# Weight roundings queued behind the PSUM evictions already written, and a layer's first two projections in the scores' banks

## The chip, the cores and the metric

The kernel runs on one core of a Trainium2 chip. The metric is the time of one execution on the device, in microseconds (us). The unchanged kernel ("before") was run three times: 1394.19, 1395.66 and 1396.37 us, median 1395.66.

A core has a matrix engine (TensorE, here PE), a vector engine (DVE), a scalar engine (ACT), GpSimd (POOL) and a sync engine (SP), which issues the large DMAs. Each takes its own instructions from its own queue in order, and waits for the others through semaphores. Matrix products accumulate in PSUM, eight banks of 128 partitions x 512 f32; everything else works from SBUF.

## The reference, cut to what matters

Two layers of an encoder over 512 tokens of width 1024, in f32:

```python
for l in range(2):
    h = rms_norm(x, norm_mix[l])
    q, k, v, gq, gk, gv = split(h @ w_in[l])            # 8 neighbourhood heads, 8 grouped queries on 2 KV heads
    na = neighbourhood_attention(q, k, v, rpb[l])       # softmax over windows of 8 rows x 16 columns
    ga = gqa_block_attention(rope(rms_norm(gq)), rope(rms_norm(gk)), gv)
    x = x + concat(na, ga) @ w_out[l]
    x = x + memory_cross_attention(rms_norm(x), rms_norm(mem), ...)   # 4 heads over 256 memory tokens
    x = x + conv_ffn(rms_norm(x), ...)                  # SwiGLU, width 2816, depthwise convolution of width 3
return rms_norm(x, norm_final)
```

## The kernel before

**Products in three parts.** Each f32 operand is held as two reduced-precision tiles (type F32R): `hi`, the rounded value, and `lo`, the rest. `mm3` forms a product as hi·hi + hi·lo + lo·hi, three matmuls into one bank. So a weight that comes by DMA (`raw`) must be rounded and its rest formed before PE can use it. This is `emit_split` (L249 to L266): `act.copy(hi, raw)` on ACT (L264, shown as `hi<-raw`) and `tensor_sub(lo, raw, hi)` on POOL or DVE (L265, `lo<-raw,hi`). Most weights of the attentions and all FFN weights are 128x1024; those of the attentions are cut in two, so a weight gives two copies and two subtractions of 128x512.

**When a weight is rounded.** `plan` lists all weights in the order of their use. `get_w` takes the next one and, on the way, calls `emit_split` for the one two places further on (five at most), and starts the DMAs of the next raw tiles. The program thus writes a weight's rounding well before its use, in the middle of the other work.

**What sets the order.** PE and SP keep the order in which the program writes their instructions. ACT, DVE and POOL do not: a planner places their instructions by a priority (the place in the program, moved by `behind(n)`) and by its own estimate of when operands are ready. Once the program is built, each engine's order is fixed. In before, a weight's rounding has `behind(45)`, so it may slide behind later work or stand ahead of it, as the planner finds ACT free.

**What takes results out of PSUM.** Most products leave their bank in the same two steps as the weights, hi on ACT and lo on DVE:

- `split_psum` (L469 to L475): softmax weights after their transposes (ACT L471, DVE L472) and v (L474, L475);
- `split_k` (L660 to L669): ACT L663, DVE L667; in layer 0's first key also a doubled copy;
- `split_q` (L678 to L683): ACT L681, DVE L683;
- `gqa_rope` (L831 to L889) for the grouped queries and the key: ACT L839 (times a gain) and L840 (square), DVE L841, then `swap` (a transposing product with `pairs` on PE, DVE L851 and L854), `rotate` (POOL L861 to L864), `norm` (a product with `ident` on PE, into a new bank) and `split` (DVE L874, then `split_q` or `split_k`).

A bank comes free when the last of these has read it.

**PSUM banks.** Three groups of tiles: `mm` with four banks (`ps_mm`), `sc` with two (`ps_s`, scores), `tr` with two (`ps_t`, transposes). A group hands its banks out in turn.

**The attentions.** In layer 0 `project_first` (L606) runs the first three projections q0, k0 and q1 interleaved, as x and the weights arrive; in layer 1 `project_qk` (L631) runs them one by one. Then come, woven together by hand-written schedules: the neighbourhood heads (`na_scores`, DVE L738 and ACT exponentials L744; `na_normalise`, L750, L756 and POOL L478; `na_transpose`; `na_values`, ACT L788 and DVE L789, L790), with the grouped projections as filler; then the grouped heads (`gqa_scores`, DVE L899 for the maximum and ACT L901 for the exponential; `gqa_normalise`, DVE L907 and POOL L478; `gqa_transpose_p`, transposes on PE and `split_psum`; `gqa_values`), with the output projection `out_na` (DVE L956 adds it to x) and the memory attention's preparation (ACT L539, L524; POOL L523; DVE L540) as filler. The memory attention and the conv-FFN follow. In time, layer 0's attention lies at about 25 to 241 us and layer 1's at about 705 to 924.

Of the kernel before, what the change touches and what calls it, by code (L numbers as in the profile page):

```python
# [12 lines left out]
AF = mybir.ActivationFunctionType  # L13
# [159 lines left out]
def encoder_kernel(ctx: ExitStack, tc: tile.TileContext, t: dict, out: bass.AP):  # L173
# [14 lines left out]
    @contextmanager  # L188
    def behind(n):


        at = tc.cur_priority
        tc.cur_priority = at + n
        yield
        tc.cur_priority = at
# [30 lines left out]
    ps_mm = lambda: ps("mm", 4)  # L226
# [5 lines left out]
    plan, raws, ready = [], [], []  # L232
    done = [0]

    def raw_tile():
        key, loads, nk, ncol, eng = plan[len(raws)]
        if eng[1:] == "x":
            raw = rtile((nk, ncol), F32)
        else:
            raw = wpool.tile([P, nk, ncol], F32, tag="raw", name=nm("raw"), bufs=N_RAW)  # L240
        raws.append(raw)
        return raw, loads
# [6 lines left out]
    def emit_split(act=ACT, cuts=2):  # L249
        n = len(ready)  # L250
        key, loads, nk, ncol, eng = plan[n]
        raw = raws[n]
        raws[n] = None
        if key[0] in ("up", "down", "memq", "memo"):
            cuts = 1
        if eng[1:] == "r":
            hi, lo = rtile((nk, ncol)), rtile((nk, ncol))
        else:
            hi = wpool.tile([P, nk, ncol], F32R, tag="hi", name=nm("hi"))
            lo = wpool.tile([P, nk, ncol], F32R, tag="lo", name=nm("lo"))  # L260
        with behind(W_BEHIND if done[0] and key[0] not in ("up", "down") else 0):
            for i in range(cuts):
                k = slice(nk * i // cuts, nk * (i + 1) // cuts)
                act.copy(hi[:, k], raw[:, k])  # L264
                (POOL if eng[0] == "P" else DVE).tensor_sub(lo[:, k], raw[:, k], f(hi)[:, k])  # L265
        ready.append((hi, lo))  # L266

# [200 lines left out]

    def split_psum(hi, lo, ps, scale=None):  # L469
        if scale is None:  # L470
            ACT.copy(hi, ps)  # L471
            DVE.tensor_sub(lo, ps, f(hi))  # L472
        else:
            ACT.mul(hi, ps, scale)  # L474
            DVE.scalar_tensor_tensor(lo, ps, scale, f(hi), op0=ALU.mult, op1=ALU.subtract)  # L475

    def normalise(e, sums, col, eng=DVE):
# [110 lines left out]
    for l in range(DEPTH):  # L588
# [11 lines left out]
        def project_first():  # L600

            w, pms = {}, {}
            for u, k0, k1 in ((0, 0, 2), (1, 0, 2), (0, 2, 4), (1, 2, 4), (2, 0, 4), (0, 4, 6),
                              (1, 4, 6), (2, 4, 6), (0, 6, 8), (1, 6, 8), (2, 6, 8)):
                if u not in w:
                    w[u], pms[u] = get_w(NA_ORDER[u]), ps_mm()  # L606
                if (u, k0) == (0, 0):

                    for k in range(2):
                        PE.matmul(pms[u], w[u][0][:, k], xg[k][0], start=k == 0, stop=False)  # L610
                        PE.matmul(pms[u], w[u][0][:, k], xg[k][1], start=False, stop=False)
                    for k in range(2):
                        PE.matmul(pms[u], w[u][1][:, k], xg[k][0], start=False, stop=False)
                    continue
                gemm_T(pms[u], w[u], xg, range(k0, k1), 0, KC - 1)
            load_bias(0)
            load_parameters()
            mix.stat()

            def evict():  # L620
                mix.spread()
                for u in range(3):
                    split_qk(*NA_ORDER[u], pms[u])

            late(1, evict)
            yield
# [2 lines left out]

        def project_qk(n, p):  # L630
            w = get_w((n, p))  # L631
            pm = ps_mm()
            gemm_T(pm, w, xg, range(0, 4), 0, KC - 1)
            yield
            gemm_T(pm, w, xg, range(4, 8), 0, KC - 1)
            if (n, p) == ("q", 0):
                mix.stat()
                held.append(pm)
            elif (n, p) == ("k", 0):
                mix.spread()  # L640
                split_qk("q", 0, held.pop())
                split_qk("k", 0, pm)
            else:
                split_qk(n, p, pm)
            yield
# [14 lines left out]
        def split_k(pm, kt, near):  # L660
            rows = [(slice(64 * j, 64 * j + 64), slice(64 - 64 * j, 128 - 64 * j)) for j in range(2)]
            for k, (r, o) in zip(kt, rows):
                ACT.copy(k[r, 0], pm[r])  # L663
                if near:
                    ACT.copy(k[o, 0], pm[r])
            for k, (r, o) in zip(kt, rows):
                DVE.tensor_sub(k[r, 1], pm[r], f(k[r, 0]))  # L667
                if near:
# [9 lines left out]
        def split_q(pm, st):  # L678
            halves = [(st[:, j], slice(64 * j, 64 * j + 64), slice(64 - 64 * j, 128 - 64 * j)) for j in range(2)]
            for v, r, o in halves:  # L680
                ACT.copy(v[r], pm[r])  # L681
            for v, r, o in halves:
                DVE.tensor_sub(v[o], pm[r], f(v[r]))  # L683

# [149 lines left out]
        def gqa_rope(g, pm):  # L834
# [2 lines left out]
            xs, sq, cc = tmp(), tmp(), tmp()  # L837
            with behind(-20):
                ACT.activation(xs, pm, AF.Copy, scale=gain)  # L839
                ACT.activation(sq, pm, AF.Square)  # L840
                DVE.scalar_tensor_tensor(cc, pm, gain, gtab[0][:, 0], op0=ALU.mult, op1=ALU.mult)  # L841

            def swap():
# [290 lines left out]
        ffn = nn  # L1134
# [222 lines left out]
```

## Time and profile before

| | |
|---|---|
| time, three runs | 1394.19, 1395.66, 1396.37 us (median 1395.66) |
| profiled execution | 1398.05 us |
| its span, first to last instruction | 1396.3 us |
| mean granted TensorE clock | 0.993 |
| busy PE, DVE, ACT, POOL | 1357.5, 832.4, 710.3, 719.2 us |
| HBM read, written | 125.00 MB, 2.10 MB |

The profile is one execution. In the lines quoted below, L264 is line 264 of the kernel; `out<-in` gives the tiles by the program's names. A timeline line has the start and the length in us, the engine, the line, the operation, the tiles and shapes, the number of instructions drawn together, and in square brackets how long the engine had been idle and what released it (the releaser is inferred). Where several instructions are drawn together the length is that of all of them.

### The profile page before, as it was taken

To read this page: it belongs to the slowest core of one execution; us is meant where nothing else is said; L and a number is where in the kernel's file an instruction comes from. 1 tells how busy PE (TensorE), PEld (TensorE's weight loads), DVE (VectorE), ACT (ScalarE), POOL (GpSimd) and SP (SyncE) were. 2 spreads that over 40 slices of the span, in tenths; PEclk is the share of its full clock that TensorE was granted. 3 is DMA by queue.
4 is the path that set the end of the run, shared out by engine and by line. 5 is a ranking of instruction groups with operands and counts; after the bars stand their busy time and mean duration, and the time that the engine had idled before them with its cause. 6 is when DMAs were issued, how large, how long until landed. Compare 5 with 4: busy or idle time off the path is not lost.

```text
span 1396.3 us, 19216 instructions
## 1 busy us (share of the span) xinstructions
PE 1357.5 (97%) x7088; PEld 1158.8 (83%) x7088; DVE 832.4 (60%) x1422; ACT 710.3 (51%) x1323; POOL 719.2 (52%) x537
## 2 busy tenths in 40 slices
PE   8999899989999999999999989999999999999997
PEld 7997789878888888888888878897788888888897
DVE  6666766364687178357446657753638843871873
ACT  6676577655443234234557657765554422432443
POOL 2458776634544443444645678756264444444441
PEclk9999999999999999999999999999999999999999
DMA  7653312422333333333355523223133333333331
GB/s 216 177 148 97 87 46 65 117 61 61 91 106 92 104 91 95 102 91 96 97 160 161 137 75 98 62 76 106 42 95 91 105 91 93 101 93 106 89 93 61
DMA packets 218205, 138.83 MB, mean 99 GB/s; under 512 B 6016, under 2 KB 211072, under 8 KB 218112
## 3 DMA queue, kind: packets, MB, share of 16 engines
q1 hardware_dynamic: 217968, 137.60, 34.3%
q8 instruction: 56, 0.92, 0.3%
q14 instruction: 37, 0.30, 0.1%
q10 hardware_dynamic: 144, 0.00, 0.0%
HBM read 125.00 MB, written 2.10 MB: 91 GB/s over the span
## 4 chain that ended last, share of the span: by engine, by line
PE 88%; DVE 4%; ACT 4%; issue 2%; DMA 1%; POOL 1%; SPq 0%; DVEq 0%; ACTq 0%
PE mm L76 80%; PE sc L76 3%; PE tr L63 3%; PE tr L76 1%; DMA raw<-in_w_in 1%; ACT hi L264 1%; DVE r L472 1%; ACT t L744 1%; POOL lo L265 0%; DMA xT<-in_xT 0%; ACT t L840 0%; DVE t L841 0%; DVE s L899 0%; ACT t L839 0%; DVE xg L472 0%
## 5 line engine op out<-in xcount | busy, mean ns | idle before, releaser
L265 POOL TENSOR_TENSOR lo<-raw,hi 128x1024 fp32r<-128x1024 f32 (+2 forms) x268 | 499.6, 1875 | 505.0 <-ACT hi L264 477.4
L76 PE MATMUL mm<-xg,hi 128*128 128x512 f32 x1984 | 617.1, 392 | 4.5 <-DVE t L841 2.9
L76 PEld LDWEIGHTS mm<-xg,hi 128*128 128x128 f32 x1984 | 369.9, 189 | 80.0 <-DVE t L841 3.3
L264 ACT CAST hi<-raw 128x512 fp32r<-128x512 f32 (+2 forms) x276 | 224.4, 836 | 345.0 <-PE mm L76 289.2
L76 PE MATMUL mm<-xg,lo 128*128 128x512 f32 x992 | 387.4, 391 | 0.0
L76 PE MATMUL mm<-r,hi 128*128 128x512 f32 (+1 forms) x1160 | 336.4, 374 | 2.5 <-DVE r L472 2.0
L76 PEld LDWEIGHTS mm<-r,hi 128*128 128x128 f32 x1160 | 210.5, 189 | 41.0 <-DVE r L472 2.8
L1181 DVE SCALAR_TENSOR_TENSOR t<-t,par,t 128x7 f32<-128x7 f32 (+1 forms) x352 | 201.9, 640 | 34.3 <-ACT t L1174 34.3
L76 PEld LDWEIGHTS mm<-xg,lo 128*128 128x128 f32 x992 | 187.0, 189 | 39.6
L76 PE MATMUL mm<-r,lo 128*128 128x512 f32 (+1 forms) x580 | 216.4, 373 | 0.0
L76 PEld LDWEIGHTS mm<-r,lo 128*128 128x128 f32 x580 | 109.4, 189 | 19.3
L1166 DVE TENSOR_TENSOR t<-mm,rep 128x512 f32<-128x512 f32 x88 | 60.1, 687 | 78.2 <-PE mm L76 61.9
L478 POOL TENSOR_SCALAR t<-t,s 128x512 f32<-128x512 f32 (+1 forms) x112 | 65.8, 602 | 77.8 <-DVE s L750 40.4
L1183 ACT ACTIVATE t<-t 128x512 f32<-128x512 f32 x44 | 27.9, 633 | 134.4 <-DVE t L1181 134.4
L1187 DVE TENSOR_TENSOR r<-t,r 128x512 fp32r<-128x512 f32 x44 | 90.2, 2051 | 7.3 <-ACT r L1186 4.1
L1210 DVE TENSOR_TENSOR xT<-xT,mm 128x512 f32<-128x512 f32 x32 | 21.9, 685 | 106.8 <-PE mm L76 106.8
L76 PE MATMUL sc<-r,r 128*128 128x256 f32 (+1 forms) x352 | 72.2, 336 | 4.1 <-DVE r L472 1.8
L63 PE MATMUL tr<-ident,t 128*128 128x128 f32 x456 | 62.9, 274 | 11.2 <-DVE r L472 3.8
L63 PEld LDWEIGHTS tr<-ident,t 128*128 128x128 f32 x456 | 52.3, 140 | 20.2 <-issue 7.9
L1174 ACT ACTIVATE t<-t,par 128x512 f32<-128x512 f32 x88 | 66.8, 806 | 3.3 <-DVE t L1166 3.3
L76 PE MATMUL mm<-r,r 128*128 128x256 f32 (+1 forms) x428 | 62.5, 297 | 0.0
L76 PEld LDWEIGHTS sc<-r,r 128*128 128x128 f32 x352 | 51.4, 190 | 10.0 <-ACT r L471 3.0
(136 smaller groups left out, 1541.8 us busy)
## 6 DMA issues: line engine op xcount, KB each, us to landing
raw<-in_w_up SPq DMA_DIRECT2D x88, 512.0 KB, 3.9
raw<-in_w_in SPq DMA_DIRECT2D x33, 512.0 KB, 4.6
raw<-in_w_down SPq DMA_DIRECT2D x32, 448.0 KB, 3.8
raw<-in_w_mem_kv SPq DMA_DIRECT2D x16, 512.0 KB, 3.9
raw<-in_w_down SPq DMA_DIRECT2D x16, 512.0 KB, 4.2
r<-in_bias SPq DMA_DIRECT2D x16, 384.0 KB, 5.6
r<-r SPq DMA_DIRECT2D x22, 256.0 KB, 5.3
raw<-in_w_out SPq DMA_DIRECT2D x8, 512.0 KB, 3.7
```

The costliest lines, as they stand in the source:

```text
L63: return lambda *a, **k: self.tc.keep_in_program_order(op(*a, **k))
L76: return self.tc.keep_in_program_order(self.engine.matmul(out, lhsT, rhs, **k))
L264: act.copy(hi[:, k], raw[:, k])
L265: (POOL if eng[0] == "P" else DVE).tensor_sub(lo[:, k], raw[:, k], f(hi)[:, k])
L472: DVE.tensor_sub(lo, ps, f(hi))
L478: eng.tensor_scalar(e, e, sums[:, col : col + 1], 1.0, op0=ALU.mult, op1=ALU.mult)
L1166: DVE.tensor_mul(u, us[side], ffn.rep)
L1174: ACT.activation(cc, u, AF.Identity, bias=par[:, l, CB + ch : CB + ch + 1], scale=w[1])
L1181: DVE.scalar_tensor_tensor(cc[:, dst], u[:, src], wi, cc[:, dst], op0=ALU.mult, op1=ALU.add)
L1183: ACT.activation(cs[0], cs[0], AF.Silu)
L1187: DVE.tensor_sub(acts[j][1], cs[0], f(acts[j][0]))
L1210: DVE.tensor_add(xT[m], xT[m], pm)
```

## The change

A dictionary `evicted` holds the last ACT eviction written so far of two kinds: "other" (from `split_psum`) and "projection" (from `split_k`, `split_q` and the square in `gqa_rope`). When a weight that is not one of the FFN's is rounded, each copy on ACT is written inside `tc.issue_after(e)` for both: on ACT's queue it must stand behind those evictions. This is an edge of order only, with no semaphore, since both ends are on ACT. The roundings of the FFN's weights ("up", "down") are left as they were.

Besides, the first two projections of a layer take their banks from the scores' group: q0 and k0 of `project_first` in layer 0, q0 and k0 of `project_qk` in layer 1 (there `p` is 0 for both).

```diff
@@ -232,6 +232,9 @@
     plan, raws, ready = [], [], []
     done = [0]
 
+
+    evicted = {}
+
     def raw_tile():
         key, loads, nk, ncol, eng = plan[len(raws)]
         if eng[1:] == "x":
@@ -258,10 +261,14 @@
         else:
             hi = wpool.tile([P, nk, ncol], F32R, tag="hi", name=nm("hi"))
             lo = wpool.tile([P, nk, ncol], F32R, tag="lo", name=nm("lo"))
-        with behind(W_BEHIND if done[0] and key[0] not in ("up", "down") else 0):
+        ffn = key[0] in ("up", "down")
+        with behind(W_BEHIND if done[0] and not ffn else 0):
             for i in range(cuts):
                 k = slice(nk * i // cuts, nk * (i + 1) // cuts)
-                act.copy(hi[:, k], raw[:, k])
+                with ExitStack() as after:
+                    for e in evicted.values() if not ffn else ():
+                        after.enter_context(tc.issue_after(e))
+                    act.copy(hi[:, k], raw[:, k])
                 (POOL if eng[0] == "P" else DVE).tensor_sub(lo[:, k], raw[:, k], f(hi)[:, k])
         ready.append((hi, lo))
 
@@ -468,10 +475,10 @@
 
     def split_psum(hi, lo, ps, scale=None):
         if scale is None:
-            ACT.copy(hi, ps)
+            evicted["other"] = ACT.copy(hi, ps).ins
             DVE.tensor_sub(lo, ps, f(hi))
         else:
-            ACT.mul(hi, ps, scale)
+            evicted["other"] = ACT.mul(hi, ps, scale).ins
             DVE.scalar_tensor_tensor(lo, ps, scale, f(hi), op0=ALU.mult, op1=ALU.subtract)
 
     def normalise(e, sums, col, eng=DVE):
@@ -603,7 +610,7 @@
             for u, k0, k1 in ((0, 0, 2), (1, 0, 2), (0, 2, 4), (1, 2, 4), (2, 0, 4), (0, 4, 6),
                               (1, 4, 6), (2, 4, 6), (0, 6, 8), (1, 6, 8), (2, 6, 8)):
                 if u not in w:
-                    w[u], pms[u] = get_w(NA_ORDER[u]), ps_mm()
+                    w[u], pms[u] = get_w(NA_ORDER[u]), ps_s() if u < 2 else ps_mm()
                 if (u, k0) == (0, 0):
 
                     for k in range(2):
@@ -629,7 +636,7 @@
 
         def project_qk(n, p):
             w = get_w((n, p))
-            pm = ps_mm()
+            pm = ps_mm() if p else ps_s()
             gemm_T(pm, w, xg, range(0, 4), 0, KC - 1)
             yield
             gemm_T(pm, w, xg, range(4, 8), 0, KC - 1)
@@ -660,9 +667,10 @@
         def split_k(pm, kt, near):
             rows = [(slice(64 * j, 64 * j + 64), slice(64 - 64 * j, 128 - 64 * j)) for j in range(2)]
             for k, (r, o) in zip(kt, rows):
-                ACT.copy(k[r, 0], pm[r])
+                e = ACT.copy(k[r, 0], pm[r])
                 if near:
-                    ACT.copy(k[o, 0], pm[r])
+                    e = ACT.copy(k[o, 0], pm[r])
+            evicted["projection"] = e.ins
             for k, (r, o) in zip(kt, rows):
                 DVE.tensor_sub(k[r, 1], pm[r], f(k[r, 0]))
                 if near:
@@ -678,7 +686,7 @@
         def split_q(pm, st):
             halves = [(st[:, j], slice(64 * j, 64 * j + 64), slice(64 - 64 * j, 128 - 64 * j)) for j in range(2)]
             for v, r, o in halves:
-                ACT.copy(v[r], pm[r])
+                evicted["projection"] = ACT.copy(v[r], pm[r]).ins
             for v, r, o in halves:
                 DVE.tensor_sub(v[o], pm[r], f(v[r]))
 
@@ -837,7 +845,7 @@
             xs, sq, cc = tmp(), tmp(), tmp()
             with behind(-20):
                 ACT.activation(xs, pm, AF.Copy, scale=gain)
-                ACT.activation(sq, pm, AF.Square)
+                evicted["projection"] = ACT.activation(sq, pm, AF.Square).ins
                 DVE.scalar_tensor_tensor(cc, pm, gain, gtab[0][:, 0], op0=ALU.mult, op1=ALU.mult)
 
             def swap():
```

The number of instructions of each engine stays the same, and so does PE's order.

## The prediction, made before the changed kernel ran

> **What bounds the kernel now.** I read the page first (busy times, chain of waits, groups), then the windows by stage, then PE's timeline for its gaps, then the other engines' timelines at each gap.
>
> ```profile
> PE 1357.5 (97%) x7088; PEld 1158.8 (83%) x7088; DVE 832.4 (60%) x1422; ACT 710.3 (51%) x1323; POOL 719.2 (52%) x537
> ...
> PE 88%; DVE 4%; ACT 4%; issue 2%; DMA 1%; POOL 1%; SPq 0%; DVEq 0%; ACTq 0%
> ```
>
> PE is busy 97% of 1396.3 us, and 88% of the last chain is PE's. The time can move only through PE's 38.8 idle us and through its clock. ACT, where the moved roundings run, is about half idle. The windows by stage (columns: length, then busy us of PE, PEld, DVE, ACT, POOL, the granted clock, DMA share) say where PE waits:
>
> ```profile
> 25.00:241.00 216.00, 204.34 (x1293) 182.39 (x1292) 139.71 (x294) 145.04 (x337) 141.32 (x157) 0.98 0.40 110
> ...
> 705.00:924.00 219.00, 211.18 (x1328) 188.10 (x1328) 135.10 (x289) 144.68 (x336) 141.21 (x156) 0.99 0.39 108
> ```
>
> The two attention stages, the only ones in which the change holds a rounding back for long, idle 11.7 and 7.8 of PE's 38.8 us. The conv-FFN, whose weights the change leaves out, lies between them. PE's timeline shows the gaps, layer 0 and then layer 1:
>
> ```profile
> 34.54 0.36 PE L76 MATMUL mm<-hi,xg 128*128 128x256 f32 x1 [1.85 <-DVE r L683]
> 120.81 0.50 PE L76 MATMUL mm<-xg,hi 128*128 128x512 f32 x1 [1.43 <-DVE t L841]
> 139.39 0.63 PE L63 MATMUL tr<-ident,t 128*128 128x128 f32 x4 [1.90 <-DVE r L472]
> 149.58 1.05 PE L76 MATMUL tr<-pairs,t 128*128 128x2 f32 x8 [1.32 <-ACT t L840]
> 164.41 0.63 PE L63 MATMUL tr<-ident,t 128*128 128x128 f32 x4 [1.67 <-POOL r L523]
> 166.21 0.73 PE L76 MATMUL sc<-r,r 128*128 128x512 f32 x2 [0.70 <-ACT t L901]
> ...
> 807.59 0.73 PE L76 MATMUL mm<-xg,hi 128*128 128x512 f32 x2 [1.43 <-DVE t L841]
> 826.17 0.52 PE L63 MATMUL tr<-ident,t 128*128 128x128 f32 x3 [1.91 <-DVE r L472]
> 837.96 0.38 PE L76 MATMUL tr<-pairs,t 128*128 128x2 f32 x2 [1.33 <-ACT t L840]
> 851.27 0.63 PE L63 MATMUL tr<-ident,t 128*128 128x128 f32 x4 [1.63 <-DVE xg L472]
> 851.65 1.18 PE L76 MATMUL sc<-r,r 128*128 128x512 f32 x4
> ```
>
> The same four places come back 686.8 us later. Call them A (34.54), B (120.81, 807.59), C (139.39, 826.17), D (149.58, 837.96) and E (164.41 to 166.21, 851.27). One thing more costs PE time, its clock:
>
> ```profile
> 151.00:154.00 3.00, 3.00 (x12) 2.57 (x11) 0.20 (x2) 0.00 (x0) 3.00 (x5) 0.52 0.53 131
> 826.97:830.38 3.41, 3.41 (x10) 2.63 (x9) 2.07 (x3) 1.51 (x3) 2.12 (x2) 0.50 0.09 20
> ```
>
> The granted clock is halved in these two stretches, and in a third of the same kind behind A. The second row is cut to its edges: 3.41 us at 0.50, about 1.7 us lost by each, some 5 in the profiled execution. Each comes right after a gap (A, D of layer 0, C of layer 1).
>
> **The change part by part.** Nothing is added or removed: the same roundings, evictions, matmuls and DMAs. PE's order is the same, SP's queue all but the same. What moves is the order on ACT, and through it on DVE and POOL, since the planner places them all. All three take their queues in order, so each moved instruction is a possible new wait. With the changed program's order beside the old one, I carried the durations of the rows through at A to E.
>
> *Roundings as such.* A pair takes about 1.14 us on ACT (the 135.53 and 147.19 rows below), its subtractions follow on POOL or DVE. Queued behind the evictions, weights come 2 to 12 us later; in before they are ready well ahead, and I found no first use overtaken. Cost taken 0; bounds 0 and +2.3 (one such pair of stretches, 1.14 each, late once). Cover gone, the matmul waits for that pair.
>
> *A, the banks.* With q0 and k0 in the scores' two banks, the third projection's successor (the first v block) finds a free bank, and the 1.85 us gap goes. But the first scores then wait for k0's last subtraction in that same bank, which was not on the path: v's block is done about 2 us earlier and the subtractions are not. The gap moves behind the v block. Bounds −1.85 and +0.3; I take −0.2, nearest to a mere move. In layer 1 there is no such gap, 0.
>
> *C and D: the intended gain.*
>
> ```profile
> 135.53 1.14 ACT L264 CAST hi<-raw 128x512 fp32r<-128x512 f32 x2 [1.75 <-PE mm L76]
> ...
> 147.19 1.14 ACT L264 CAST hi<-raw 128x512 fp32r<-128x512 f32 x2
> 148.35 0.69 ACT L839 ACTIVATE t<-mm,qkg 128x512 f32<-128x512 f32 x1
> 148.94 0.59 ACT L840 ACTIVATE t<-mm 128x512 f32<-128x512 f32 x1
> ```
>
> Here a rounding pair stands ahead of the rotary eviction L839/L840, which PE waits for directly (D), or over L841 and L472 (C). The change puts the pair behind. L839 then starts about where the pair started, which itself had waited for nothing but a 0.1 us overlap (D) or the projection's end (C). Of 1.14 I count −0.95 at D and −1.0 at C, in each layer.
>
> *B: a loss.* In the changed program the key eviction L663 stands ahead of the four exponentials L744 and of L839/L840; before, it came last.
>
> ```profile
> 117.30 0.48 ACT L744 ACTIVATE t<-sc,s 128x256 f32<-128x256 f32 x1
> ...
> 118.54 0.70 DVE L874 TENSOR_TENSOR mm<-t,mm 128x512 f32<-128x512 f32 x1 [0.45 <-PE mm L76]
> ...
> 121.44 1.41 DVE L667 TENSOR_TENSOR r<-mm,r 64x512 fp32r<-64x512 f32 x2 [0.68 <-ACT r L663]
> 123.33 0.68 DVE L789 TENSOR_TENSOR t<-mm,t 64x512 f32<-64x512 f32 x1 [0.48 <-POOL t L864]
> ...
> 120.23 1.17 ACT L663 CAST r<-mm 64x512 fp32r<-64x512 f32 x2
> 121.43 1.19 ACT L788 COPY t<-mm 64x512 f32<-64x512 f32 x2
> ...
> 124.48 1.16 PE L63 MATMUL tr<-ident,t 128*128 128x128 f32 x8
> ```
>
> L663 needs L874, done at 119.24, so ACT stands still until then: L663 pair to 120.4, three exponentials (0.47 each) to 121.8, L839 and L840 to 123.0, the last exponential and a rounding pair to 124.6, and L788 ends at 125.8 instead of 122.6. Behind it are DVE's two L789 (0.69) and the small L851 that frees the bank for PE's second transpose group: 126.85, where PE wanted it at 125.0 (half of the eight from 124.48). The stall at 120.81 itself becomes 1.1 longer (its bank is now freed by the two L667), but that is inside the 1.85. B: +1.9 per layer; bounds −1.4 and +2.5.
>
> *E: the largest term.* Before:
>
> ```profile
> 156.50 0.39 PE L76 MATMUL mm<-r,lo 128*128 128x512 f32 x1
> ...
> 155.38 1.17 ACT L681 CAST r<-mm 64x512 fp32r<-64x512 f32 x2 [4.52 <-DVE mm L874]
> 156.58 0.69 ACT L901 ACTIVATE t<-sc,s 128x512 f32<-128x512 f32 x1
> ...
> 158.01 0.69 DVE L956 TENSOR_TENSOR xT<-xT,mm 128x512 f32<-128x512 f32 x1
> 158.62 0.16 DVE L907 RECIPROCAL s<-s 128x2 f32<-128x2 f32 x1
> ...
> 158.87 1.36 POOL L478 TENSOR_SCALAR t<-t,s 128x512 f32<-128x512 f32 x2 [1.22 <-DVE s L907]
> ...
> 156.37 1.28 POOL L864 TENSOR_TENSOR t<-t,t 128x512 f32<-128x512 f32 x1
> ...
> 161.29 0.59 ACT L471 CAST xg<-tr 128x512 fp32r<-128x512 f32 x1
> 161.78 2.01 ACT L539 ACTIVATE r<-r 128x1024 f32<-128x1024 f32 x2
> ...
> 843.33 0.39 PE L76 MATMUL mm<-r,lo 128*128 128x512 f32 x1
> 846.06 1.84 POOL L523 TENSOR_SCALAR r<-r,par 128x256 f32<-128x256 f32 x4
> 848.64 0.71 ACT L524 CAST r<-r 128x256 fp32r<-128x256 f32 x2
> ```
>
> Changed order: on DVE the residual add L956, which must wait for the output projection's last matmul (156.89), stands ahead of L874; on ACT, L681 (needs L874) stands ahead of the exponentials L901; on POOL, L864 stands behind L478 of those exponentials; the next L874 needs that L864; and on ACT the next L681 and both L539 stand ahead of L471 and the next L901. From 156.89 this gives one chain: L956 0.69, L874 0.70, L681 1.17, L901 pair 1.36, L907 0.16, L478 pair 1.36, L864 1.28, L874 0.70, L681 1.17, L539 pair 2.01, L471 0.59, L901 0.69, L471 0.59, L901 0.69: 13.2, and some 0.4 of hand-overs, 13.6. The second score matmul, which needs the bank that the last L901 frees, would start at 170.5 where it started at 166.21: +4.3. In layer 1 the same chain has three L523 (0.46 each) ahead of L864 and two L524 (0.71) in place of L539, and one L471 less: 11.9 and 0.4, from 843.72 to 856.0, against 852.20 (half of the 1.18 after 851.65): +3.8. Bounds for each: −1.6 (the gap goes and no chain forms) and +5.5.
>
> *Clock.* I leave the three half-clock stretches as they are: those after C and D may go, two longer gaps at E may bring theirs. Bounds −5.1 and +3.4. The Trainium skill (TensorE: Matmul & The Clock Gate, What's actually happening) says that the window of 3413 ns runs free of the kernel and that the clock halves after at least one idle window. The length agrees with the 3.41 above; that an idle window is needed does not, since no gap here exceeds 1.91. By that rule only E's new gaps would halve the clock.
>
> *Sum.* Layer 0: −0.2 + 1.9 − 1.0 − 0.95 + 4.3 = +4.05. Layer 1: 1.9 − 1.0 − 0.95 + 3.8 = +3.75. Together +7.8 on the profiled execution's 1398.05 (span 1396.3), which is 2.4 above the median of the runs, 1395.66. The part that is the chip's phase (clock stretches) explains that much, so I add the sum to the median: 1403.5.
>
> **The rivals.**
> 1. *Faster: the chains at B and E don't form, C and D shrink.* For it: C and D point straight at roundings in ACT's queue. Against: in before, every start at E follows from in-order queues to within 0.05 us (L681 155.38 right behind L874, L901 156.58 right behind L681), so a changed order must bite. It decides if L956 or L681 comes earlier than I have it. Price: 2 × (−1.95) and up to one gap at E, −0.7: 1391.
> 2. *No change.* B and E lose just what C, D and the clock stretches give back, for instance E +1.2 each where POOL's L864 isn't the link that lasts: about +2.4 + 3.8 − 4.1 − 0.2, less a clock stretch: 1396.
> 3. *Worse: the clock follows.* Each gap over 3.4 us at E brings a half-clock stretch of 1.7 and the old ones stay, or a weight comes late: 1403.5 + 3.4 = 1407. By the skill's rule above it would be this one.
> 4. *The change doesn't do what it says.* The edge is only one of issue order and could leave the order alone; the orders differ in both attentions, so no chance of its own.
>
> **How the numbers follow.** A difference under 0.2% (2.8 us) can't be told from none here. Forecast (1400 to 1405.5) 0.54, rival 1 0.20, rival 2 0.12, rival 3 0.14. Faster 0.20, within 0.2% 0.12, slower 0.68. The likeliest case's own range is 1399 to 1407; to leave out no more than 2 in 10 it must reach into rival 2 and to the top of rival 3: 1393.5 to 1408. Predicted 1403.5.
>
> **What would show it.** In the changed profile: PE gaps at C and D about 1 us shorter; a gap over 3 us in front of a transpose or a score matmul at about 165 to 171 and 850 to 857, released by ACT t L901 or DVE xg L472; ACT idle before L681 there, released by DVE mm L874; ACT idle before L663 at about 118, released by DVE mm L874; the window 25 to 245 with over 14 us of PE idle. Wrong if E's gaps stay under 2 us, or if a matmul waits on POOL lo L265 or ACT hi L264.

## The result, and the profile after

| | before | after |
|---|---|---|
| median of the runs made together, us | 1396.01 (4 runs, 1394.19 to 1400.53) | 1415.18 (4 runs, 1412.52 to 1417.83) |
| ratio, with 95% interval | | 1.0123 [1.0104, 1.0142] |
| profiled execution, its span, us | 1398.05, 1396.3 | 1417.22, 1415.4 |
| mean granted clock of it | 0.993 | 0.987 |

The changed kernel is 1.2% slower, some 19 us. The forecast had the direction, 1403.5, but 1415.18 lies outside its range of 1393.5 to 1408.

The page of the changed kernel, busy times and the chain that ended last:

```profile
PE 1367.6 (97%) x7088; PEld 1166.6 (82%) x7088; DVE 834.7 (59%) x1422; ACT 710.2 (50%) x1323; POOL 720.0 (51%) x537
...
PE 84%; DVE 4%; POOL 4%; ACT 3%; DMA 3%; issue 2%; SPq 1%; DVEq 0%; ACTq 0%; POOLq 0%
```

The counts of instructions are those of before, and ACT and POOL are busy as long as they were. PE's idle time went from 38.8 to 47.8 us (1415.4 − 1367.6), and PE's busy time, for the same 7088 matmuls, from 1357.5 to 1367.6. So there are two losses of about 9 and 10 us: PE waits longer, and it works more slowly. In the chain POOL rose from 1% to 4% and DMA from 1% to 3%.

The windows of the changed kernel over the same two attention stages (columns as in the prediction):

```profile
25.00:241.00 216.00, 199.57 (x1236) 176.91 (x1235) 137.35 (x287) 139.91 (x324) 134.58 (x149) 0.98 0.38 105
705.00:924.00 219.00, 206.34 (x1217) 182.30 (x1217) 125.69 (x267) 133.43 (x307) 131.33 (x144) 0.96 0.37 106
```

PE idles 16.4 us of the first and 12.7 us of the second, where it had idled 11.7 and 7.8: 4.8 us more in each. The clock of the second stage fell from 0.99 to 0.96. PE's timeline in the changed kernel shows the gaps that answer to A to E, layer 0 and then layer 1:

```profile
122.77 0.70 PE L76 MATMUL mm<-xg,hi 128*128 128x512 f32 x2 [2.63 <-DVE r L675]
129.99 0.69 PE L63 MATMUL tr<-ident,t 128*128 128x128 f32 x4 [1.36 <-DVE s L859]
145.04 0.66 PE L63 MATMUL tr<-ident,t 128*128 128x128 f32 x4 [0.94 <-DVE r L479]
164.74 2.08 PE L76 MATMUL mm<-ident,t 128*128 128x128 f32 x8 [3.31 <-POOL t L870]
173.23 0.63 PE L63 MATMUL tr<-ident,t 128*128 128x128 f32 x4 [2.17 <-DVE xg L479]
...
780.92 0.36 PE L76 MATMUL mm<-hi,xg 128*128 128x256 f32 x1 [1.81 <-DVE r L482]
818.58 0.70 PE L76 MATMUL mm<-xg,hi 128*128 128x512 f32 x2 [2.63 <-DVE r L675]
860.72 0.70 PE L76 MATMUL mm<-ident,t 128*128 128x128 f32 x2 [3.47 <-POOL t L870]
870.08 0.50 PE L76 MATMUL sc<-r,r 128*128 128x512 f32 x1 [2.03 <-ACT t L909]
```

(Lines of the changed kernel are 7 to 8 further on than before's: its rounding is L271 and L272, the rotary eviction L847 and L848, `rotate` L869 to L872, the normalised product's DVE step L882, the transposes' eviction L478 and L479.) C fell from 1.90 to 0.94 (145.04) and D from 1.32 to 0.42. B rose from 1.43 to 2.63 (122.77), with a second gap of 1.36 behind it (129.99). E has 3.31 and 2.17 in place of 1.67 and 0.70. At 780.92, in the middle of layer 1's second v projection, stands a gap that the prediction didn't have (called the v block below; layer 0 has 0.59 at the same place, 86.66).

The same stretch of the other three engines at E of layer 0, in the changed kernel:

```profile
161.50 1.17 ACT L689 CAST r<-mm 64x512 fp32r<-64x512 f32 x2 [4.80 <-DVE mm L882]
...
160.12 0.69 DVE L964 TENSOR_TENSOR xT<-xT,mm 128x512 f32<-128x512 f32 x1 [0.53 <-PE mm L76]
160.72 0.69 DVE L882 TENSOR_TENSOR mm<-t,mm 128x512 f32<-128x512 f32 x1
...
167.30 0.70 DVE L882 TENSOR_TENSOR mm<-t,mm 128x512 f32<-128x512 f32 x1 [2.95 <-POOL t L872]
...
153.07 1.29 POOL L506 TENSOR_TENSOR r<-t,r 128x512 fp32r<-128x512 f32 x1 [1.08 <-ACT r L505]
154.38 1.28 POOL L871 TENSOR_TENSOR t<-t,r 128x512 f32<-128x512 f32 x1
...
156.17 2.53 POOL L272 TENSOR_TENSOR lo<-raw,hi 128x512 fp32r<-128x512 f32 x2
158.65 1.29 POOL L872 TENSOR_TENSOR t<-t,t 128x512 f32<-128x512 f32 x1
...
164.07 0.62 POOL L870 COPY t<-s 128x512 f32<-128x512 f32 x1
```

ACT stands still for 4.80 us ahead of L689, as forecast. DVE's L882, which it waits for, is queued behind the residual add L964, as forecast too; but its operand from POOL's L872 was itself done only at 159.94 (158.65 + 1.29), because a rounding's two subtractions (2.53) now stand in POOL's queue ahead of it. The add costs 0.8 there. From then on POOL is the late one: PE waits for its L870, done at 164.69, and the next L882 for its L872.

The remaining loss is the clock. Windows of the changed kernel, laid on the edges of the half-clock stretches: three pairs, each the 3.41 us ahead of a stretch and the stretch itself, and between them one window (171.38) that no half clock follows:

```profile
120.18:123.59 3.41, 0.82 (x4) 0.71 (x5) 1.38 (x2) 3.37 (x10) 2.08 (x2) 1.00 0.63 191
123.59:127.00 3.41, 3.41 (x10) 2.63 (x9) 0.83 (x2) 3.00 (x8) 1.34 (x2) 0.50 0.18 42
127.01:130.42 3.41, 2.05 (x19) 1.80 (x17) 2.11 (x5) 0.89 (x2) 3.41 (x5) 1.00 0.00 0
130.42:133.83 3.41, 3.41 (x10) 2.72 (x9) 2.41 (x4) 2.14 (x4) 3.30 (x3) 0.50 0.56 163
...
171.38:174.79 3.41, 1.56 (x9) 1.41 (x10) 2.95 (x6) 3.34 (x9) 3.41 (x8) 1.00 0.00 0
778.95:782.36 3.41, 1.60 (x14) 1.47 (x13) 0.48 (x1) 3.41 (x11) 2.92 (x3) 1.00 0.45 133
782.36:785.77 3.41, 3.41 (x18) 3.41 (x18) 2.45 (x5) 2.75 (x7) 2.21 (x4) 0.50 0.66 196
```

There are eight such stretches in this execution, from 123.59, 130.42, 164.55, 782.36, 819.91, 826.74, 860.87 and 871.11, against four of before (from 35.08, 151.13 and 826.97, and one at the start of the kernel, from 7.8). Each lasts 3.41 us at 0.50, so it loses about 1.7 us, and all starts lie on one grid: from 123.59 to 871.11 it is 219 steps of 3.413 us. The 3.41 us ahead of each of the eight hold a gap of PE, with 0.15 us (from 857.46) to 2.05 us (from 127.01) of work beside it. Before's stretch at the start cost little: after has none there, and its 101st matmul starts at 26.7 us where before's starts at 27.0. Both executions also end at half clock, from 1390.2 us in before and from 1407.0 in after, when PE has next to nothing left to do.

**The loss in two parts.** Every run has its span and its mean clock, so the clock's loss is span × (1 − clock): for the changed kernel 1413.4 × (1 − 0.9878) = 17.3 us, as means over its four runs. Span less this loss is called the rest here. Some 3 us of every clock loss (2.5 to 4.3 in the fourteen profiled executions) are the end of the execution, where half clock costs next to nothing; so of the two columns only differences are read. In the table, in us:

| kernel | runs | clock loss | rest |
|---|---|---|---|
| before (each batch of runs) | 15 to 23 | 7.1 to 8.1 | 1388.2 to 1388.4 |
| after | 4 | 17.3 | 1396.1 |
| banks only | 12 | 9.2 | 1388.8 |
| order only | 4 | 15.9 | 1395.0 |
| behind "other" only | 4 | 12.3 | 1397.8 |
| behind "projection" only | 4 | 16.3 | 1396.8 |
| POOL's steps behind the rotation | 4 | 17.7 | 1400.0 |
| output weights' rests on DVE | 4 | 13.8 | 1399.8 |
| first grouped weights free | 4 | 16.3 | 1396.7 |
| two weights only | 11 | 6.5 | 1388.2 |
| two weights, rests on DVE | 12 | 9.1 | 1388.6 |
| one weight | 12 | 9.7 | 1388.3 |
| after, gaps filled | 4 | 7.0 | 1399.3 |
| before, gaps filled | 12 | 5.1 | 1389.5 |

The rest scatters from run to run: four runs of one kernel lie within 1.9 us of each other at best and 7.9 at worst (output weights' rests on DVE), so a mean over four is good to one or two us. After less before (7.6 and 1388.2 in 23 runs): the rest grew by 7.9, the clock's loss by 9.7.

### The profile page after: what moved, and what is told of

It reads as the page before. It is cut to its first block, busy times and chain, and to the rows that moved or that the text cites. A ratio compares the mean times of both kernels' runs of the same rounds, so it can differ in the third digit from the quotient of the medians.

```text
span 1415.4 us, 19196 instructions
## 1 busy us (share of the span) xinstructions
PE 1367.6 (97%) x7088; PEld 1166.6 (82%) x7088; DVE 834.7 (59%) x1422; ACT 710.2 (50%) x1323; POOL 720.0 (51%) x537
## 4 chain that ended last, share of the span: by engine, by line
PE 84%; DVE 4%; POOL 4%; ACT 3%; DMA 3%; issue 2%; SPq 1%; DVEq 0%; ACTq 0%; POOLq 0%
PE mm L76 77%; PE sc L76 4%; PE tr L63 3%; POOL lo L272 2%; DMA raw<-in_w_in 1%; PE tr L76 1%; DMA t<-t 1%; ACT hi L271 1%; SPq L63 1%; POOL t L485 0%; DVE r L479 0%; DMA xT<-in_xT 0%; DVE xg L479 0%; DVE s L907 0%; POOL t L872 0%
## 5 line engine op out<-in xcount | busy, mean ns | idle before, releaser
L272 POOL TENSOR_TENSOR lo<-raw,hi 128x1024 fp32r<-128x1024 f32 (+2 forms) x268 | 500.2, 1877 | 541.7 <-ACT hi L271 519.7
L76 PE MATMUL mm<-xg,hi 128*128 128x512 f32 x1920 | 599.1, 393 | 5.3 <-DVE r L675 5.3
L76 PEld LDWEIGHTS mm<-xg,hi 128*128 128x128 f32 x1920 | 359.2, 189 | 77.8 <-issue 5.6
L76 PE MATMUL mm<-xg,lo 128*128 128x512 f32 x960 | 376.1, 392 | 0.0
L271 ACT CAST hi<-raw 128x512 fp32r<-128x512 f32 (+2 forms) x276 | 224.3, 840 | 301.0 <-PE mm L76 246.3
L76 PEld LDWEIGHTS mm<-xg,lo 128*128 128x128 f32 x960 | 181.6, 189 | 38.6
```

Source lines behind the costliest of these rows:

```text
L76: return self.tc.keep_in_program_order(self.engine.matmul(out, lhsT, rhs, **k))
```

## The experiments

Theories ahead of the runs: the order on ACT's queue causes it all, through DVE and POOL (the rival: the banks); POOL's order makes E's gaps (the rival: DVE's residual add); a rounding that waits for its DMA stands ahead of v's eviction; the half clock follows PE's gaps (the rival: it varies by itself). Each kernel had one profiled run and timed rounds beside before on the same chip.

**1. The banks alone.** The edges are taken out, the banks stay changed.

```diff
-                with ExitStack() as after:
-                    for e in evicted.values() if not ffn else ():
-                        after.enter_context(tc.issue_after(e))
-                    act.copy(hi[:, k], raw[:, k])
+                act.copy(hi[:, k], raw[:, k])
```

> The two bank lines alone; every engine's order stays that of before. Theory Q (the loss is the new order on ACT, DVE and POOL, and the clock follows the gaps it makes): within 3 us of before (1393 to 1399), PE idle 37 to 40 us, two to four half-clock stretches, and the 1.85 us gap ahead of the first v block gone or moved to the first scores. Rival B (the banks do it: the rotation of the four general banks shifts, and PE waits for a later reader at 120 us): over 1400, with the gaps at about 120 and 807 us above 2 us.

Measured 1399.34 against 1398.83, ratio 1.0012 [1.0000, 1.0023]. Its PE timeline behind the first v block:

```profile
36.99 0.38 PE L76 MATMUL sc<-r,r 128*128 128x256 f32 x1 [1.54 <-DVE r L669]
```

Before's gap of 1.85 at 34.54 is gone and two gaps, 1.54 and 1.14, stand behind the v block, in front of the first score products, which wait for the key's last subtraction in the bank that they need. The gap moved, as step A has it. The banks add at most 0.2%; they are not the cause.

**2. The order alone.** The banks are taken back, the edges stay.

```diff
-                    w[u], pms[u] = get_w(NA_ORDER[u]), ps_s() if u < 2 else ps_mm()
+                    w[u], pms[u] = get_w(NA_ORDER[u]), ps_mm()
...
-            pm = ps_mm() if p else ps_s()
+            pm = ps_mm()
```

> The queue edges alone, with all projections in the general banks; ACT's, DVE's and POOL's order is that of the changed kernel. Theory Q: as the changed kernel, 1411 to 1418, PE idle 46 to 50 us, gaps of about 2.6 us at 120 and 3.3 us at 161 and the same two in layer 1. Rival B: 1396 to 1404.

Measured 1412.53, ratio 1.0103 [1.0088, 1.0119]. Its PE timeline has the changed kernel's gaps, 2 us earlier in time:

```profile
120.55 0.81 PE L76 MATMUL mm<-xg,hi 128*128 128x512 f32 x2 [2.63 <-DVE r L675]
...
162.38 2.07 PE L76 MATMUL mm<-ident,t 128*128 128x128 f32 x8 [3.21 <-POOL t L870]
```

The edges alone carry the loss, as far as these runs can tell, and in both parts (rest 1395.0, clock loss 15.9).

**3 and 4. Only one kind of edge.** Behind the evictions of "other" alone, or of "projection" alone, with before's banks.

```diff
-                    for e in evicted.values() if not ffn else ():
+                    for e in [v for n, v in evicted.items() if n == "other"] if not ffn else ():
```

> As e2, but a rounding is held only behind the last eviction of transposes and v blocks, not behind projections. Theory Q with the losses shared by both kinds of edge: 1400 to 1409. If one kind carries the whole loss, one of e3 and e4 is at 1411 or more and the other within 3 us of before.

> As e2, but a rounding is held only behind the last eviction of a projection. At C and D it is the projection's eviction that the rounding stood ahead of, so the gaps at 137 and 148 us shrink by 1 us each as in the changed kernel. Theory Q with shared losses: 1400 to 1412; the gap at the residual add (about 161 us) over 2 us if the projection edge makes it.

Measured 1412.06, 1.0098 [1.0083, 1.0114], and 1415.22, 1.0122 [1.0100, 1.0144]. The loss isn't shared out between the two kinds: either one alone costs nearly the whole. PE's timeline with "other" alone, then with "projection" alone:

```profile
122.01 2.08 PE L76 MATMUL mm<-ident,t 128*128 128x128 f32 x8 [2.65 <-POOL t L870]
```

```profile
169.62 1.09 PE L63 MATMUL tr<-ident,t 128*128 128x128 f32 x4 [4.25 <-DVE xg L479]
```

Both disturb the same stretches, but in another way each: "other" alone makes PE wait for POOL at B (2.65, for a rotation's L870) and again at E, "projection" alone makes one long wait for ACT and DVE. So the loss does not hang on one of the two kinds; either gives the planner another order of the three engines. That is not so for every later rounding: with one or two weights (8 to 10 below) the waits cost nothing in sum.

**5. POOL's order at E.** If POOL's queue were only in a bad order, the rounding's subtractions and the normalised weights' (L506) could be held behind the rotation.

```diff
-                (POOL if eng[0] == "P" else DVE).tensor_sub(lo[:, k], raw[:, k], f(hi)[:, k])
+                with ExitStack() as after:
+                    if eng[0] == "P" and rot[0] is not None and not ffn:
+                        after.enter_context(tc.issue_after(rot[0]))
+                    (POOL if eng[0] == "P" else DVE).tensor_sub(lo[:, k], raw[:, k], f(hi)[:, k])
...
-                POOL.tensor_add(xr, cc, xr)
+                rot[0] = POOL.tensor_add(xr, cc, xr).ins
```

(and the same wrap around L506, `POOL.tensor_sub(lo, o32, f(hi))`.)

> The changed kernel, and on POOL each subtraction of a rounding (and that of a neighbourhood head's output) is held behind the rotation products already written. Theory P (at E POOL is late: a rounding's pair of subtractions, 2.5 us, and a waiting L506 stand ahead of the rotation that PE needs): the 3.3 us gaps at 161 and 857 us released by POOL shrink below 1 us, 4 to 9 us faster than the changed kernel with their half-clock stretches. Theory D (the residual add ahead of L882 on DVE, as predicted): the chain over ACT stays, a gap over 3 us at 161 to 172, at most 2 us faster.

Measured 1418.87, 1.0165 [1.0151, 1.0179]: slower still. Its PE timeline:

```profile
162.64 0.50 PE L76 MATMUL mm<-r,hi 128*128 128x512 f32 x1 [2.82 <-POOL r L512]
...
166.90 1.16 PE L76 MATMUL mm<-ident,t 128*128 128x128 f32 x8 [2.15 <-POOL t L876]
```

PE now waits for what was put back (L512 is the shifted L506), and for the rotation as well. In both orders that were tried POOL is late at E with something. The edge holds the subtractions back wherever a rotation has been written, not at E alone, so the time prices all of that; that this order of POOL mends nothing is shown, that no order would is not.

**6. Less work on POOL.** The rests of the output projection's weights go to DVE.

```diff
-            cols(("outn", mp), w_out, 0, 4, 256 * mp, 256, "P")
+            cols(("outn", mp), w_out, 0, 4, 256 * mp, 256, "D")
```

> The changed kernel with the rests (lo) of the four neighbourhood output-projection weights made on DVE (0.65 us each) instead of POOL (1.27 us): the queue edges stay, the 2.5 us of POOL ahead of the rotation go. Theory P: the gaps released by POOL at 161 and 857 us shrink by 2 us or more, 3 to 8 us faster than the changed kernel. Theory D: within 2 us of it, or slower, since DVE gets 1.4 us more ahead of L882.

Measured 1415.68, 1.0138 [1.0122, 1.0153], no gain. Its PE timeline at E:

```profile
172.17 1.22 PE L76 MATMUL sc<-r,r 128*128 128x512 f32 x2 [2.80 <-ACT t L909]
```

PE still waits for POOL, 2.62 in place of 3.31, and then longer for ACT, 2.80 in place of 2.17.

**7. The v block's gap.** The weights of the grouped key and of the first grouped query are left without edges.

```diff
-                    for e in evicted.values() if not ffn else ():
+                    for e in evicted.values() if not ffn and key not in (("g", "k"), ("g", 0)) else ():
```

> The changed kernel, but the weights of the grouped key and of the first grouped query are rounded without the edges. Theory M (in the second v projection a rounding waits on ACT for its DMA, 4.0 us in layer 1, and the eviction of v behind it holds PE's bank): the gaps at 86 (0.6) and 779 us (1.8) go, with the half clock after the second; 2 to 5 us faster than the changed kernel. If the v gap stays and no rounding waits there for a DMA, M is wrong.

The mechanism in the changed kernel itself first, at the v block of layer 1, ACT, DVE and then PE (whose row stands above, 780.92):

```profile
778.74 1.14 ACT L271 CAST hi<-raw 128x512 fp32r<-128x512 f32 x2 [3.96 <-DMA raw<-in_w_in]
779.79 0.47 ACT L481 ACTIVATE r<-mm,s 128x256 fp32r<-128x256 f32 x1
...
780.29 0.48 DVE L482 SCALAR_TENSOR_TENSOR r<-mm,s,r 128x256 fp32r<-128x256 f32 x1 [3.34 <-ACT r L481]
```

ACT stands 3.96 us in front of a rounding whose raw tile has not landed; behind it in the queue is v's eviction L481, then DVE's L482, and PE needs the bank that this frees. Measured: 1414.32, 1.0131 [1.0117, 1.0145]. In layer 0 the gap of 0.59 at 86.66 shrank to 0.30 (87.38), but at 81.43 one of 0.45 came, where PE waits for a weight's rest on POOL; in layer 1 it shrank from 1.81 to 1.44, but ACT waits as before:

```profile
777.27 1.14 ACT L271 CAST hi<-raw 128x512 fp32r<-128x512 f32 x2 [3.99 <-DMA raw<-in_w_in]
```

So the mechanism is visible, the cure was incomplete, and the time shows nothing of it. Whether the DMA could be made to start earlier, with one more raw tile, was not tried.

**8. Two weights alone.** Edges only for the two output weights that stood ahead of C and D, and before's banks.

```diff
-                    for e in evicted.values() if not ffn else ():
+                    for e in evicted.values() if key in (("outn", 2), ("outn", 3)) else ():
```

> The queue edges for two weights of each layer alone, the third and fourth of the neighbourhood output projection, which stand ahead of the rotary evictions at C and D in before; general banks. Gain theory: C and D shrink by 1 us each per layer and POOL keeps the rotation ahead: PE idle 34 to 36 us, 1390 to 1395. Theory P would let a gap at E grow by up to 2 us per layer, since the rounding's pair on POOL still moves: 1394 to 1400.

Measured 1396.37 against 1396.87, 0.9997 [0.9989, 1.0006]. In its PE timeline C fell from 1.90 to 1.63 and D from 1.32 to 0.41, but E grew:

```profile
155.18 1.16 PE L76 MATMUL mm<-ident,t 128*128 128x128 f32 x8 [0.77 <-POOL t L870]
163.25 1.08 PE L63 MATMUL tr<-ident,t 128*128 128x128 f32 x4 [3.29 <-POOL r L530]
```

What C and D give, E takes; the rest is before's 1388.2 to 0.1 us.

**9 and 10. Smaller still.** One weight alone, or these two with their rests on DVE, both with before's banks.

```diff
-                    for e in evicted.values() if not ffn else ():
+                    for e in evicted.values() if key == ("outn", 3) else ():
```

> The queue edges for one weight of each layer, the fourth of the neighbourhood output projection (D). The gaps at 148 and 837 us shrink by 0.9 us as in e5. If e5's new idle time at E came from the third weight's pair of subtractions, pushed on POOL from 136 us to behind the output projection, E stays as in before: PE idle 36.5 to 37.5 us, 1391 to 1395. If any rounding that leaves the rotary eviction's way meets it again at E, E grows by 1 us as in e5: 1394 to 1398.

> e5 with the rests of these two weights made on DVE, not on POOL. If POOL is what E waits for, E's growth in e5 (+1.5 and +1.2 us) goes and C's and D's gain stays: PE idle 35 to 37 us, 1391 to 1395. If E is bound by the chain over ACT and DVE, DVE's extra 1.4 us per weight makes it no better than e5: 1395 to 1399.

Measured 1400.60, 1.0018 [1.0008, 1.0029], and 1399.28, 1.0014 [1.0006, 1.0023], both a little slower. Their rest is before's (1388.3 and 1388.6); what grew is the clock's loss, 9.7 and 9.1 against 7.6. With one weight D is again 0.41 and a gap of 2.08 comes at E. With the rests on DVE, POOL's gaps at E are 0.30 and 1.66, and in layer 0 DVE is late in POOL's place:

```profile
176.90 0.98 PE L76 MATMUL tr<-ones,t 128*128 128x1 f32 x4 [5.90 <-DVE s L915]
```

**11. The changed kernel with its gaps filled.** PE gets idle matmuls (512 columns, into a transposes' bank that nobody reads) in front of the grouped v projection, 10, and of the last query's product with `ident`, 12, in each layer. The waits stay; PE is busy in them.

```diff
+    FEED = InOrder(tc, nc.tensor)
...
+        def feed(n):
+            d = ps_t()
+            for _ in range(n):
+                FEED.matmul(d, xg[0][0][:, 0:P], xg[0][0], start=True, stop=True)
...
+            if g == "v":
+                feed(10)
...
+                if g == 3:
+                    feed(12)
```

> The changed kernel with idle matmuls put on PE where it waits: 10 of 512 columns ahead of the grouped v projection (the 2.63 us gaps at 120 and 816 us) and 12 ahead of the last query's norm product (the 3.3 us gaps at 161 and 857), into a transpose bank that nobody reads. They add about 2.3 and 2.8 us of work that fits into the waits. Theory C (a half-clock stretch follows a gap of PE): the stretches right after these four gaps (124, 165, 820, 861) go, up to four of the eight, so 3 to 7 us faster than the changed kernel although the waits themselves stay. Rival R (the stretches come with the code there or at random): as many stretches, the time within 2 us of the changed kernel or longer.

Measured 1407.92, 1.0082 [1.0054, 1.0109]; some 6 to 7 us faster than the changed kernel (the two intervals overlap by a hair, 1.0104 to 1.0109) with 44 matmuls more (the two groups of layer 0 take 2.46 and 2.88 us, so about 10.7 us in all). Its PE timeline and its windows over the two stages:

```profile
118.13 2.46 PE L63 MATMUL tr<-xg 128*128 128x512 f32 x10
120.92 0.70 PE L76 MATMUL mm<-xg,hi 128*128 128x512 f32 x2 [0.34 <-DVE r L676]
...
156.34 2.88 PE L63 MATMUL tr<-xg 128*128 128x512 f32 x12
160.13 1.16 PE L76 MATMUL mm<-ident,t 128*128 128x128 f32 x8 [0.92 <-POOL t L878]
```

```profile
25.00:241.00 216.00, 204.67 (x1296) 181.56 (x1297) 141.36 (x293) 143.06 (x333) 139.79 (x154) 1.00 0.38 108
705.00:924.00 219.00, 211.10 (x1300) 186.70 (x1299) 134.56 (x284) 139.79 (x323) 134.19 (x149) 0.99 0.37 104
```

The waits are there, worked through instead of idled: B's 2.63 became 2.46 of idle matmuls and 0.34 of wait, E's 3.31 became 2.88 and 0.92. The half-clock stretches of the profiled execution went from eight to one (from 859.57), and over the runs the clock's loss went from 17.3 to 7.0, which is before's, while the rest rose by 3.2.

Of the seven stretches that went, four had followed the gaps now filled (123.59, 164.55, 819.91, 860.87). The one at the v block of layer 1 went together with its gap, though nothing was put there: ACT waits 1.13 us for the DMA there in place of 3.96, so the order on the engines changed as well. The two behind B's second gap went although that gap stayed (1.35 at 126.53 and at 816.84). The one that is left follows a gap of 2.09 (858.34) that was not filled. So a filled gap draws no half clock, and a gap that stays may or may not; some 10 us of clock loss went with the fill, not all of it provably by the fill.

**12. Before with its gaps filled.** The same for the unchanged kernel: 7 idle matmuls in front of layer 0's first v block (A), 5 in front of the last query's product with `pairs` (D) in each layer (`feed` is given the bank here).

```diff
+            if (l, g) == (0, 0):
+                feed(ps_t(), 7)
...
                 pv = ps_t()
+                if g == 3:
+                    feed(pv, 5)
```

> The kernel before, with idle matmuls on PE in two of its own waits: 7 ahead of layer 0's first v block (the 1.85 us gap at 34 us) and 5 ahead of the last query's sum of squares in each layer (the 1.3 us gaps at 149 and 838 us). Theory C: the half-clock stretches that follow 34 and 149 us in before (35 and 151) go, 1.7 us each, and the fill costs nothing while it fits into the wait: 1.5 to 4 us faster than before, 1393 to 1397 against 1397 to 1398 of the runs beside it. Rival R: no fewer stretches, the same time, or slower by the fill's 0.2 us per matmul (up to 4 us).

Measured 1396.16 against 1398.51, 0.9989 [0.9980, 0.9997]: the lowest ratio of all, 0.1% under before, which is just clear of the noise, and about 19 us under the changed kernel. Its PE timeline at A, and windows where before had its stretches of layer 0, with the one that is left:

```profile
32.42 1.75 PE L63 MATMUL tr<-xg 128*128 128x512 f32 x7
34.72 0.36 PE L76 MATMUL mm<-hi,xg 128*128 128x256 f32 x1 [0.55 <-DVE r L684]
```

```profile
35.00:38.40 3.40, 3.19 (x27) 2.98 (x25) 3.06 (x5) 3.33 (x6) 2.26 (x2) 1.00 0.34 102
...
140.49:143.90 3.41, 3.41 (x10) 2.67 (x9) 2.07 (x3) 1.47 (x3) 2.15 (x2) 0.50 0.09 19
151.00:154.40 3.40, 3.20 (x22) 2.71 (x21) 1.27 (x4) 1.72 (x5) 3.40 (x4) 1.00 0.34 77
```

Full clock behind A and D, and one stretch behind C, which was not filled (in before it was C of layer 1 that had one, not C of layer 0). The idle matmuls cost 1.1 us of the rest and spare 2.7 of clock loss.

## Why the prediction was right or wrong

The delays between the same matmuls of both profiled executions, added up by place, stand beside its terms:

| step | predicted, us | wait measured, layer 0 and layer 1 |
|---|---|---|
| A, the banks | −0.2 | about 0 |
| roundings as such | 0 (bounds 0 and +2.3) | +0.74 and +1.38, at the v blocks |
| B | +1.9 each | +2.44 and +2.55 |
| C and D | −1.95 each | −1.86 and −1.87 |
| E | +4.3 and +3.8 | +2.95 and +3.75 |
| clock | 0 (bounds −5.1 and +3.4) | +9.7 in the runs |

**The waits.** A, C and D came as worked out. B has the mechanism of the prediction (ACT stands 5.68 us in front of the key's eviction, released by DVE's L882), a little dearer:

```profile
120.01 1.17 ACT L670 CAST r<-mm 64x512 fp32r<-64x512 f32 x2 [5.68 <-DVE mm L882]
```

The gap in front of the v projection grew by 1.20 (to 2.63), as the step had it (1.1). The second gap, in front of the transposes, is 1.36, where the step's 1.85 left 0.75 for it. DVE's two evictions of the values (L797, before's L789) were to start behind ACT's L796; by the releaser that the profile names they started only when PE's products with `pairs` had ended, and L859, which frees the bank, stands behind them:

```profile
128.25 1.40 DVE L797 TENSOR_TENSOR t<-mm,t 64x512 f32<-64x512 f32 x2 [3.55 <-PE tr L76]
```

E's size is right in layer 1 and 1.35 too high in layer 0, and its chain is half right. The step began the chain with the residual add, which is there but costs only 0.8; the link that lasts is POOL's, whose rotation stands behind a waiting subtraction and a rounding's pair. The prediction had listed L864's place behind L478 but not that pair. Its sign, a gap over 3 us in front of a transpose or a score matmul, released by L901 or L472, did not come: the gaps over 3 us (3.31 and 3.47) stand in front of the product with `ident` and are released by POOL's L870. Only the smaller ones behind them (2.17 and 2.03) have the releasers it named. In layer 1 the steps it lists add up to 12.7, not 11.9 (13.2 + 3 × 0.46 − 2.01 + 0.71 − 0.59), which would have made the term +4.6; that +3.8 came so near +3.75 is in part luck.

"Roundings as such" at 0 failed at the v blocks: it looked for a first use overtaken, and the loss is that the rounding itself waits, for its DMA (2.56 us in layer 0, 3.96 in layer 1), with v's eviction behind it.

All terms together gave +7.8 and the rest grew by 7.9, but that match is luck: the waits in the table add up to +10.1, some −0.7 came later, and PE's idle time grew by 9.0. B and the roundings were too low and E too high, and the rest is good to one or two us only.

**The step that failed** is the clock: "I leave the three half-clock stretches as they are". The term was 0 with +3.4 as its bound, and the runs showed +9.7: the loss grew from 7.6 to 17.3. (In the two profiled executions it is eight stretches of 1.7 us against three that cost, +8.5.) That is most of the 11.7 us between 1403.5 and 1415.2. Rival 3 named the mechanism, but let only the gaps over 3.4 us at E bring a stretch. The rows of before already spoke against this: its own gaps of 1.85, 1.32 and 1.91 had each brought one, while others of 1.33 to 1.90 had not. Every new or longer gap should have had a stretch as its upper bound: two at E, two at B (one for each of its gaps), in both layers, and one or two at the v blocks, each 1.7. In the profile of after seven of the eight stretches lie at B and E and one at a v block. That a gap of PE draws them is shown by experiments 11 and 12: the four behind the gaps filled in 11 went, as did before's two at A and D in 12, and the clock's loss over the runs fell by 10.3 and 2.7. How many of the new ones are the doing of a gap alone is not shown, since in 11 three others went without a fill.

The forecast of a stalled ACT ahead of L681 and L663 and of over 14 us of PE idle in the first stage held; it said that the reasoning would be wrong if E's gaps stayed under 2 us, and they are 3.31 and 2.17. Its other sign of being wrong, a matmul that waits for a rounding's rest (L265, now L272), came once, for 0.15 us at 80.42.

**The clock rule.** In the changed kernel half clock came after 3.41 us windows that held between 0.15 (857.46) and 2.05 us (127.01) of PE work, and on one grid. The Trainium skill (TensorE: Matmul & The Clock Gate, What's actually happening) has the clock halve after at least one idle window of about 3.4 us, in a window that runs free of the kernel. The grid and the length agree with the rows. That the window must be idle does not: 1.36 us of idle was enough at 127.01. If idle means wholly idle, no half clock would have followed any of the windows shown.

**Left open.** How E's loss divides among POOL, DVE and ACT: each of experiments 5, 6, 9 and 10 took or shortened one wait there and found another. The DMA wait at layer 1's v block, which no run took away by itself. And what decides whether a gap is followed by half clock.

## What to carry to other kernels

A rounding moved on one in-order queue can take its other half on POOL or DVE, its raw tile's DMA and the planner's order of all engines with it, and a wait taken away at one engine can come back at the next, as it did here at E. When a change may open a gap of over a microsecond on a matrix engine that is 97% busy, price the gap together with the half-clock stretch that can follow (here 1.7 us each, in all about as much as the waits themselves). Where a wait can't be removed, a few idle matmuls in it can cost less than the clock that they keep (experiment 12: 1.1 us against 2.7).

## What the runs showed of the hardware

Half clock came after windows of the 3.41 us grid with only 1.3 to 2 us of idle PE, and not always. Two windows of before, the first followed by half clock and the second not:

```profile
147.72:151.13 3.41, 2.09 (x14) 1.58 (x13) 2.46 (x6) 3.12 (x8) 3.41 (x4) 1.00 0.16 36
...
161.37:164.78 3.41, 1.74 (x13) 1.32 (x12) 3.33 (x6) 3.41 (x6) 1.85 (x5) 1.00 0.00 0
```

The second has less PE work and kept its clock, as did the changed kernel's 171.38 (1.56). So busy time alone does not decide; what does, these runs do not settle. Nor does the same program have the same stretches in every run: of 23 runs of before the shortest span, 1391.8 us, had a mean clock of 0.997 and the longest, 1398.1, one of 0.992, and the span less the clock's loss scattered by 1.0 us (standard deviation) where the span did by 1.7.
